# S5 first states behind the first head's group norm on GpSimd, fewer VectorE operations for the S5 parameters, the last chunk's transfers ahead of weight loads, and a different split in the tail

## The chip, the cores and the metric

The program runs on one NeuronCore of a Trainium2 chip. A core has a matrix engine (TensorE, PE in the profile), three engines for elementwise work (VectorE or DVE, ScalarE or ACT, GpSimd or POOL), and a queue engine (SyncE, SP) that only issues transfers. Each engine works through its own list of instructions; they are tied together by semaphores. The metric is device time in microseconds (us), median of repeated runs. A second, profiled execution has its own time and leaves a trace of every instruction.

## The reference

One decoder layer over 256 prompt positions and 64 sample positions (8 sequences of 8), 320 columns in all, width 2048, all in float32:

```python
proj = rms_norm(x, norm_mix) @ w_in                  # 2048 -> 5120: u | q | k | v | g
# S5: 64 groups x 64 complex states, zero-order hold
lam_bar = exp(lam * dt);  b_bar = ((lam_bar - 1) / lam) * b
bu = einsum(u, b_bar);  bu[0] += lam_bar * x0        # x0 is given for the samples
xs = associative_scan(lam_bar, bu)
y  = gelu(Re(C xs) + d * u);  y = y * sigmoid(y @ w_glu + b_glu)
# retention: 8 heads, rotary, decay per head, group norm, swish gate
o  = ((q k^T) * mask) v + (q r) * decay;  o = norm(o) * gn_w * silu(g)
x  = x + concat(y, o) @ w_out
x  = x + (silu(h2 @ w_gate) * (h2 @ w_up)) @ w_ffn_out   # h2 = rms_norm(x); 2048 -> 5632 -> 2048
y_out = rms_norm(x)                                  # also returned: S5 and retention states
```

The S5 parameters that the change touches are small: `exp(lam * dt)` per state, its powers up to the fourth, and `(lam_bar - 1) / lam`, on tiles of 128 partitions by 32 pairs of groups.

## The kernel before

Activations lie transposed, features on partitions and the 320 positions along the free dimension. Every weight block is split into two parts, `hi` (rounded to the matrix engine's fast float32 form) and `lo` (the rest), and so are the activations; a product is three matmuls (hi by hi, hi by lo, lo by hi). So each weight load of 512 KB (eight blocks of 128 by 128) costs one transfer into `raw`, one ACT cast to `hi` (L133), one DVE subtraction to `lo` (L135) and 24 matmuls of 320 columns. `raw`, `hi` and `lo` have three buffers each: a transfer waits until the `lo` three loads earlier is made, a cast waits until PE has finished with the load three earlier.

The opening (L922 to L956) multiplies four column blocks together while x arrives. It goes in steps over the 16 row blocks k of x: the first two steps take one k each, then seven take two. In a step SP loads x and w_in, ACT makes `xhi` (L272), casts the weights (`hi<-raw`, L943) and squares x for the norm (L277), DVE makes `xlo` and `lo` (L273, L944), and PE does 12 matmuls per k (L953). Behind it follow the other projections, head by head: q, k, v and g for retention and one block of u for S5. Beside them run the S5 chunks (eight, `s5_chunk`), the rotary and mask work of the heads (`head_k`, `head_v`), then the output projection, the gated unit and the feed-forward part, which is most of the time.

The S5 parameters are made beside the opening. POOL computes two exponentials from a polynomial (`s5_exps`, `vexp`, L346 to L367): first the step size, then the magnitude `rr`, 23 operations of 128 by 32 each. DVE computes sine and cosine (`s5_params`), then `lp` (powers of lam_bar), `ff`, `gp` and `r4`, the fourth power of `rr` (`s5_params2`, `s5_params3`). `first_states` puts lam_bar^4 times x0 into `lx0` with six POOL operations.

The order on PE and POOL is the order in which the code is written (a simulated clock, `clk`, and a heap of generators decide when a helper's code is run). The order on ACT, DVE and SP is made by a scheduler from priorities (`tc.high_priority(offset=...)`) and its own estimates of time; `tc.issue_after(ins)` puts an instruction behind another one of the same engine only. In the tail (from L1358) all engines go in written order.

Towards the end of the projections the last S5 chunks pass data through DRAM and inside SBUF: `back` and `yc` bring a chunk's output into channel order (L678, L683), and six small transfers `toe<-toe` (L649) copy a Toeplitz block to other partitions, after an ACT copy (L645). The PE group `py` (L104) needs `toe`. These transfers stand on SP between the loads of w_out. In the tail, the last rows of the feed-forward output are made in token layout; `scale` and `store` write the outputs, and `keep_warm(12)` puts 12 matmuls without use in front of the last broadcast.

Of the kernel before, what the change touches and what calls it, by code (L numbers as in the profile page):

```python
# [46 lines left out]
def hybrid_kernel(ctx, tc, xT, w_in, w_in4, w_out, w_glu, w_fi, w_fo, w_fot, gfr, vecs, s5p, bc, x0,  # L47
# [335 lines left out]
    def s5_params(dt_):  # L383
        newscr(0)

        ang = T(she)
        tt(ang[:, 0], prm[:, 1], dt_, MUL)
        ts(ang[:, 1], ang[:, 0], 8.0, MUL)
        ts(ang[:, 2], ang[:, 0], 64.0, MUL)
        nn = ts(T(she), ang, float(1 / np.pi), MUL, MAGIC, ADD)  # L390
        ts(nn, nn, MAGIC, SUB)
        for part in PI_PARTS:
            stt(ang, nn, -part, ang, MUL, ADD)
        par = ts(T(she), nn, 0.5, MUL, MAGIC, ADD)
        ts(par, par, MAGIC, SUB)
        stt(par, nn, 0.5, par, MUL, SUB)
        tt(par, par, par, MUL)
        ts(par, par, -8.0, MUL, 1.0, ADD)
        a2 = tt(T(she), ang, ang, MUL)
        q = T(she)  # L400
        ts(q, a2, 1.0 / factorial(13), MUL, -1.0 / factorial(11), ADD)
        for kk in (9, 7, 5, 3, 1):
            tt(q, q, a2, MUL)
            ts(q, q, (1.0 if (kk // 2) % 2 == 0 else -1.0) / factorial(kk), ADD)
        tt(q, q, ang, MUL)
        tt(es[:, 0::3], q, par, MUL)
        q = T(she)
        ts(q, a2, -1.0 / factorial(14), MUL, 1.0 / factorial(12), ADD)
        for kk in (10, 8, 6, 4, 2, 0):
            tt(q, q, a2, MUL)  # L410
            ts(q, q, (1.0 if (kk // 2) % 2 == 0 else -1.0) / factorial(kk), ADD)
        tt(ec[:, 0::3], q, par, MUL)
        for l in range(2):
            n = (NE - 1 - l + 2) // 3
            c_, s_ = ec[:, l::3][:, :n], es[:, l::3][:, :n]
            u1, u2 = T([P, n, NPAIR]), T([P, n, NPAIR])
            tt(u1, c_, c_, MUL)
            tt(u2, s_, s_, MUL)
            tt(ec[:, l + 1::3][:, :n], u1, u2, SUB)
            stt(es[:, l + 1::3][:, :n], c_, 2.0, s_, MUL, MUL)  # L420
        s5_turns(ec, es)

    def s5_params2(used):
        newscr(1)
        scr[1] = used
        tt(lp[:, 0, 0], rr, ec[:, 0], MUL)
        tt(lp[:, 1, 0], rr, es[:, 0], MUL)
        den = tt(T(sh), prm[:, 0], prm[:, 0], MUL)
        d2 = tt(T(sh), prm[:, 1], prm[:, 1], MUL)
        tt(den, den, d2, ADD)  # L430
        rden = T(sh)
        dve.reciprocal(rden, den)
        rot_t["rden"] = rden

    def s5_params3():
        rden = rot_t["rden"]
        nr = ts(T(sh), lp[:, 0, 0], -1.0, ADD)
        t1 = tt(T(sh), nr, prm[:, 0], MUL)
        t2 = tt(T(sh), lp[:, 1, 0], prm[:, 1], MUL)
        tt(t1, t1, t2, ADD)  # L440
        tt(ff[:, 0], t1, rden, MUL)
        t3 = tt(T(sh), lp[:, 1, 0], prm[:, 0], MUL)
        t4 = tt(T(sh), nr, prm[:, 1], MUL)
        tt(t3, t3, t4, SUB)
        tt(ff[:, 1], t3, rden, MUL)
        r2 = tt(T(sh), rr, rr, MUL)
        tt(r4, r2, r2, MUL)

        def cmul(o, a, b, shape, tt=tt):

            u1, u2 = T(shape), T(shape)
            tt(u1, a[0], b[0], MUL)
# [6 lines left out]
        def ri(t, i):
            return (t[:, 0, i], t[:, 1, i])  # L460

        def rep_(t, n):
            return tuple(t[:, q].unsqueeze(1).to_broadcast([P, n, NPAIR]) for q in range(2))

        cmul(ri(lp, 1), ri(lp, 0), ri(lp, 0), sh)
        cmul(ri(lp, slice(2, 4)), rep_(lp[:, :, 1], 2), ri(lp, slice(0, 2)), [P, 2, NPAIR])
        cmul(ri(gp, slice(0, 3)), rep_(ff, 3), ri(lp, slice(0, 3)), [P, 3, NPAIR])

        def b8(a):
            return a.unsqueeze(2).to_broadcast(shx)  # L470

        def first_states():

            yield max(0.0, T0 + 12.0 - clk.now)
            newscr(0)
            cmul((lx0[:, 0], lx0[:, 1]), (x0t[:, 0], x0t[:, 1]), (b8(lp[:, 0, 3]), b8(lp[:, 1, 3])), shx,
                 pool.tensor_tensor)

        spawn(first_states())
# [99 lines left out]
    def s5_chunk(c):  # L579
# [63 lines left out]
                       start=q == 0, stop=q == 1, tile_position=(0, 64 * u))  # L643
        with tc.high_priority(offset=EVAC):
            act.copy(toe[:, :, CH - 1], pk_[:, 0:64].rearrange("p (q h) -> p q h", h=16))  # L645
        for u in range(2):
            for t in range(CH - 1):
                d = 16 * (CH - 1 - t)
                sp.dma_start(toe[64 * u + d:64 * u + 64, :, t], toe[64 * u:64 * u + 64 - d, :, CH - 1])  # L649
# [30 lines left out]
        for j in range(4):  # L680
            for g in range(2):
                r = 32 * j + 16 * g
                sp.dma_start(yc[r:r + 16], back[j % 2, :, :, j // 2, g].rearrange("t h c -> h t c"))  # L683
# [60 lines left out]
    def head_v(h, v_, qg, rt, R):  # L744
# [47 lines left out]
        pool.tensor_scalar(w_, w_, -0.5, 1.5, MUL, ADD)  # L792
        pool.tensor_tensor(y_, y_, w_, MUL)
        pool.tensor_tensor(w_, m_, y_, MUL)
# [561 lines left out]
    with tail_order:  # L1356
        act.activation(wn[:, 0:1], ones[:, 0:1], AF.Sqrt)
        ps0 = ps_tok("ps_t0")  # L1358
        mm3(ps0, 0, P, range(0, 5))
        pss = norm_ps("ps_s3")  # L1360
        for i, (s, m) in enumerate(TILES):
            pe.matmul(pss[0:m, i:i + 1], acc3[:, s:s + m], ones[:, 0:1], start=True, stop=True)
        for i, (s, m) in enumerate(TILES):
            ts(sm3[0:m, i:i + 1], pss[0:m, i:i + 1], float(D * EPS), ADD)
        mm3(ps0, 0, P, range(5, FCT))
        ps1 = ps_tok("ps_t1")
        chain(0, ps0)
# [24 lines left out]
        act.copy(rbt[1], pb1[:, 0:P])
        scale(dve, 1, 0, 5, pb1)
        scale(pool, 1, 5, 10, rbt[1])
        tok_out(1, tp_o[1], sp)
        store(1, 0, 5)
        keep_warm(12)
        x_, g_ = xo[0][0:ms_], xg[0][0:ms_]
        tt(x_, psb[0:ms_, 0:TC], xt[0:ms_, 2], ADD)
        act.activation(sqj[0:ms_], x_, AF.Square, accum_out=rs[0:ms_, 2:3])  # L1400
        scale(dve, 1, 10, NF, pb1)
        store(1, 5, 10)
        store(1, 10, NF)
# [113 lines left out]
```

## Time and profile before

| | |
|---|---|
| three runs | 1428.19, 1428.51, 1429.81 us (median 1428.51) |
| the profiled execution's own time | 1427.82 us |
| its span, first to last instruction | 1426.0 us |
| busy share DVE, ACT, POOL | 67%, 43%, 9% |
| DMA | 267.07 MB moved, mean 187 GB/s |
| granted clock of TensorE | 0.999 |

The trace has one row for each instruction, or for a few like ones in sequence: its start in us from the start of the span, its duration, engine, line, operation, the tiles written and read, their shapes, how many instructions are merged, and in brackets how long the engine had been idle before it and who ended that. "ACTq" or "SPq" marks the queue side of an engine: a transfer is issued there and lands later. Overlapping durations on one engine are pipelining, so the step from one start to the next is the cost of one.

### The profile page before, as it was taken

How to read it: one execution, taken by the hardware profiler on the slowest of the kernel's cores; microseconds unless marked ns; L12 is line 12 of the kernel's file. 1: busy time of each engine (PE TensorE's matmuls, PEld its weight loads, DVE VectorE, ACT ScalarE, POOL GpSimd, SP SyncE). 2: the span in 40 equal slices, each digit the busy share in tenths (PEclk: the TensorE clock that was granted, in tenths of full speed). 3: DMA queues.
4: the chain of work that ended last, by engine and by line, in shares of the span. 5: the costliest groups of instructions: out<-in, count | busy, mean ns of one | idle time of the engine just before them, and what ended most of it. 6: DMA issues, size and time to landing. Idle time of an engine off the chain costs nothing.

```text
span 1426.0 us, 26198 instructions
## 1 busy us (share of the span) xinstructions
PE 1416.9 (99%) x10376; PEld 1406.4 (99%) x10376; DVE 958.0 (67%) x1852; ACT 606.4 (43%) x965; POOL 124.6 (9%) x194
## 2 busy tenths in 40 slices
PE   9999999999999999999999999999999999999998
PEld 8999999999999999999999999999999999999998
DVE  7978888787657756777777545767744677645453
ACT  7645555555445443333333333333333333333452
POOL 7530021110000000000001000000000000000002
PEclk9999999999999999999999999999999999999999
DMA  8555555556544466675656446666545765455442
GB/s 289 172 170 167 159 174 154 172 163 205 169 154 149 164 207 229 222 254 199 245 201 236 136 147 240 233 213 240 167 144 183 252 230 188 154 165 179 150 142 74
DMA packets 102315, 267.07 MB, mean 187 GB/s; under 512 B 27376, under 2 KB 42160, under 8 KB 102192
## 3 DMA queue, kind: packets, MB, share of 16 engines
q1 hardware_dynamic: 101824, 264.91, 55.9%
q8 instruction: 81, 1.33, 0.4%
q10 hardware_dynamic: 368, 0.49, 0.1%
q14 instruction: 42, 0.34, 0.1%
HBM read 254.44 MB, written 10.52 MB: 186 GB/s over the span
## 4 chain that ended last, share of the span: by engine, by line
PE 76%; DVE 1%; issue 0%; ACT 0%; DMA 0%; SPq 0%; DVEq 0%; ACTq 0%
PE ps_fu L146 7%; PE ps_fg L146 7%; PE ps_fg L145 7%; PE ps_fu L145 7%; PE ps_fg L147 7%; PE ps_fu L147 7%; PE ps_fo L146 7%; PE ps_fo L145 7%; PE ps_fo L147 7%; PE ps_o L145 2%; PE ps_o L147 2%; PE ps_o L146 2%; PE ps_t L1315 1%; PE ps_g L147 1%; PE ps_g L145 1%; PE ps_g L146 1%
## 5 line engine op out<-in xcount | busy, mean ns | idle before, releaser
L133 ACT CAST hi<-raw 128x1024 fp32r<-128x1024 f32 (+1 forms) x410 | 397.8, 971 | 680.9 <-PE ps_fg L146 184.8
L135 DVE TENSOR_TENSOR lo<-raw,hi 128x1024 fp32r<-128x1024 f32 (+1 forms) x410 | 462.2, 1128 | 303.9 <-ACT hi L133 301.8
L147 PE MATMUL ps_fg<-hhi,lo 128*128 128x320 f32 x704 | 217.5, 309 | 0.0
L145 PE MATMUL ps_fg<-hhi,hi 128*128 128x320 f32 x704 | 217.5, 309 | 0.0
L146 PE MATMUL ps_fg<-hlo,hi 128*128 128x320 f32 x704 | 217.5, 309 | 0.0
L146 PE MATMUL ps_fu<-hlo,hi 128*128 128x320 f32 x704 | 217.5, 309 | 0.0
L145 PE MATMUL ps_fu<-hhi,hi 128*128 128x320 f32 x704 | 217.5, 309 | 0.0
L147 PE MATMUL ps_fu<-hhi,lo 128*128 128x320 f32 x704 | 217.5, 309 | 0.0
L145 PE MATMUL ps_fo<-ahl,hi 128*128 128x320 f32 x671 | 207.6, 309 | 0.0
L146 PE MATMUL ps_fo<-ahl,hi 128*128 128x320 f32 x671 | 207.3, 309 | 0.0
L147 PE MATMUL ps_fo<-ahl,lo 128*128 128x320 f32 x671 | 207.3, 309 | 0.0
L145 PE MATMUL ps_p<-xhi,hi 128*128 128x320 f32 x560 | 177.3, 317 | 0.0
L147 PE MATMUL ps_p<-xhi,lo 128*128 128x320 f32 x560 | 173.0, 309 | 0.0
L146 PE MATMUL ps_p<-xlo,hi 128*128 128x320 f32 x560 | 172.8, 309 | 0.0
L147 PEld LDWEIGHTS ps_fg<-hhi,lo 128*128 128x128 f32 x704 | 132.1, 188 | 0.0
L146 PEld LDWEIGHTS ps_fg<-hlo,hi 128*128 128x128 f32 x704 | 132.1, 188 | 0.0
L145 PEld LDWEIGHTS ps_fu<-hhi,hi 128*128 128x128 f32 x704 | 132.1, 188 | 0.0
L146 PEld LDWEIGHTS ps_fu<-hlo,hi 128*128 128x128 f32 x704 | 132.1, 188 | 0.0
L147 PEld LDWEIGHTS ps_fu<-hhi,lo 128*128 128x128 f32 x704 | 132.1, 188 | 0.0
L145 PEld LDWEIGHTS ps_fg<-hhi,hi 128*128 128x128 f32 x704 | 132.1, 188 | 0.0
L146 PEld LDWEIGHTS ps_fo<-ahl,hi 128*128 128x128 f32 x671 | 126.0, 188 | 0.0
L145 PEld LDWEIGHTS ps_fo<-ahl,hi 128*128 128x128 f32 x671 | 125.9, 188 | 0.0
(497 smaller groups left out, 2118.2 us busy)
## 6 DMA issues: line engine op xcount, KB each, us to landing
raw<-w_fi SPq DMA_DIRECT2D x176, 512.0 KB, 4.2
raw<-w_in SPq DMA_DIRECT2D x79, 512.0 KB, 4.1
raw<-w_fo SPq DMA_DIRECT2D x61, 512.0 KB, 3.4
raw<-w_out SPq DMA_DIRECT2D x32, 512.0 KB, 3.7
hi<-vd SPq DMA_DIRECT2D x32, 512.0 KB, 5.5
lo<-vd SPq DMA_DIRECT2D x32, 512.0 KB, 5.2
raw<-w_fo SPq DMA_DIRECT2D x61, 192.0 KB, 2.4
rt<-r SPq DMA_DIRECT2D x8, 512.0 KB, 5.6
```

The lines of the kernel that those rows point to most:

```text
L133: cast = act.copy(hi[:, :m], raw[:, :m])
L135: last_lo[0] = dve.tensor_tensor(lo[:, :m], raw[:, :m], f(hi[:, :m]), SUB)
L145: pe.matmul(ps, hi, xhi[:, k], start=k == 0, stop=False)
L146: pe.matmul(ps, hi, xlo[:, k], start=False, stop=False)
L147: pe.matmul(ps, lo, xhi[:, k], start=False, stop=k == nk - 1)
L1315: pe.matmul(ps[0:m, 0:TC], a3[:, x_, k, s:s + m], w_[:, k], start=k == 0 and x_ == 0 and w_ is whi, stop=k == FCT - 1 and w_ is wlo)
```

## The change

Five edits:

1. `s5_params`: the polynomials of sine and cosine use one fused operation per term (`stt`, scalar_tensor_tensor) in place of two.
2. `s5_params2` and `s5_params3`: the two squares for `den` move from DVE to ACT, and so do both squarings that make `r4` from `rr`; the first of them reads `rr` directly. The subtraction of 1 is fused, and the complex products are done on both parts together (`cpow`).
3. `first_states` is no longer put on the heap with a due time, but called inside head 0's group norm, behind its last POOL operation.
4. Chunk 7's six `toe` transfers and chunk 6's eight `yc` transfers get a priority of 3 x 1500.
5. Tail: the second token tile is scaled and stored in pieces of 4, 5 and 4 blocks in place of 5, 5 and 3, and 10 warm matmuls stand in place of 12.

```diff
@@ s5_params
-        q = T(she)
-        ts(q, a2, 1.0 / factorial(13), MUL, -1.0 / factorial(11), ADD)
-        for kk in (9, 7, 5, 3, 1):
-            tt(q, q, a2, MUL)
-            ts(q, q, (1.0 if (kk // 2) % 2 == 0 else -1.0) / factorial(kk), ADD)
-        tt(q, q, ang, MUL)
-        tt(es[:, 0::3], q, par, MUL)
...
+        tt(ang, ang, par, MUL)
+        for dst, top, last in ((es, 13, ang), (ec, 14, par)):
+            q = ts(T(she), a2, (-1.0) ** (top // 2) / factorial(top), MUL)
+            for kk in range(top - 2, 1, -2):
+                stt(q, q, (-1.0) ** (kk // 2) / factorial(kk), a2, ADD, MUL)
+            stt(dst[:, 0::3], q, 1.0, last, ADD, MUL)
@@ s5_params2
-        den = tt(T(sh), prm[:, 0], prm[:, 0], MUL)
-        d2 = tt(T(sh), prm[:, 1], prm[:, 1], MUL)
+        den, d2 = T(sh), T(sh)
+        act.activation(den, prm[:, 0], AF.Square)
+        act.activation(d2, prm[:, 1], AF.Square)
+        act.activation(r4, rr, AF.Square)
+        act.activation(r4, r4, AF.Square)
@@ s5_params3
-        nr = ts(T(sh), lp[:, 0, 0], -1.0, ADD)
-        t1 = tt(T(sh), nr, prm[:, 0], MUL)
+        t1 = stt(T(sh), lp[:, 0, 0], -1.0, prm[:, 0], ADD, MUL)
...
-        r2 = tt(T(sh), rr, rr, MUL)
-        tt(r4, r2, r2, MUL)
...
+        def cpow(o, a, b, n):
+            used = scr[1]
+            shn = [P, 2, n, NPAIR]
+            u1, u2 = (T([P, 2 * n, NPAIR]).rearrange("p (r n) j -> p r n j", r=2) for _ in range(2))
+            for u, q in ((u1, 0), (u2, 1)):
+                tt(u, a, b[:, q].unsqueeze(1).unsqueeze(1).to_broadcast(shn), MUL)
+            tt(o[:, 0], u1[:, 0], u2[:, 1], SUB)
+            tt(o[:, 1], u1[:, 1], u2[:, 0], ADD)
+            scr[1] = used
...
         def first_states():
-
-            yield max(0.0, T0 + 12.0 - clk.now)
             newscr(0)
...
-        spawn(first_states())
+        rot_t["first"] = first_states
@@ s5_chunk
-        for u in range(2):
-            for t in range(CH - 1):
...
+        with tc.high_priority(offset=3 * EVAC if c == 7 else 0):
+            for u in range(2):
+                for t in range(CH - 1):
+                    d = 16 * (CH - 1 - t)
+                    sp.dma_start(toe[64 * u + d:64 * u + 64, :, t], toe[64 * u:64 * u + 64 - d, :, CH - 1])
...
+        with tc.high_priority(offset=3 * EVAC if c == 6 else 0):
+            for j in range(4):
+                for g in range(2):
+                    r = 32 * j + 16 * g
+                    sp.dma_start(yc[r:r + 16], back[j % 2, :, :, j // 2, g].rearrange("t h c -> h t c"))
@@ head_v, behind the last pool operation of the group norm
+        if h == 0:
+            rot_t["first"]()
@@ tail
-        scale(dve, 1, 0, 5, pb1)
-        scale(pool, 1, 5, 10, rbt[1])
+        scale(dve, 1, 0, 4, pb1)
+        scale(pool, 1, 4, 9, rbt[1])
...
-        keep_warm(12)
+        keep_warm(10)
...
-        scale(dve, 1, 10, NF, pb1)
+        scale(dve, 1, 9, NF, pb1)
```

In all DVE has 22 instructions fewer and ACT four more; PE has two fewer (the warm matmuls) and is otherwise in the same order. `s5_params2` is called inside `tc.issue_after(turned.ins)`, where `turned` is a DVE instruction; for the four new ACT instructions that sets no place. The scheduler's order shows where they came to stand. These are ACT's rows in the opening before, from the two `xhi` of k = 10 and 11 (the first two rows) to the step of k = 12 and 13; the bracket names the semaphores that a row waits for (DMAHW are transfers):

```order
L272 ACTIVATE xhi<-retp,vec 128x320 [waits DMAHW6_49]
L272 ACTIVATE xhi<-retp,vec 128x320
L943 CAST hi<-raw 128x1024 [waits DMAHW7_49,PE_49]
L272 ACTIVATE xhi<-retp,vec 128x320 [waits DMAHW0_49]
L272 ACTIVATE xhi<-retp,vec 128x320
L277 ACTIVATE retp<-retp 128x640 [waits DVE_49]
L943 CAST hi<-raw 128x1024 [waits DMAHW1_49,PE_49]
```

and the same piece of ACT's order now:

```order
L272 ACTIVATE xhi<-retp,vec 128x320 [waits DMAHW6_49]
L272 ACTIVATE xhi<-retp,vec 128x320
L424 ACTIVATE r_126<-rr 128x32 [waits Pool_49]
L942 CAST hi<-raw 128x1024 [waits DMAHW7_49,PE_49]
L425 ACTIVATE r_126<-r_126 128x32 [waits Activation_49]
L272 ACTIVATE xhi<-retp,vec 128x320 [waits DMAHW0_49]
L272 ACTIVATE xhi<-retp,vec 128x320
L277 ACTIVATE retp<-retp 128x640 [waits DVE_49]
L942 CAST hi<-raw 128x1024 [waits DMAHW1_49,PE_49]
```

The first squaring of `rr` (L424; `r_126` is `r4`) now stands ahead of the weight cast for k = 10 and 11 and waits for POOL, which writes `rr`; the squares for `den` (L422, L423, not shown) stand two steps earlier and wait for the transfer of `prm`. On POOL, between head 0's group norm (its last two rows first) and head 1's k, the order before was

```order
L793 TENSOR_TENSOR gy<-gy 128x2
L794 TENSOR_TENSOR gy<-mv,gy 128x2
L867 COPY qsp<-q__1059 128x64
L452 TENSOR_TENSOR scrt<-x0t,lp 128x256
L453 TENSOR_TENSOR scrt<-x0t,lp 128x256
L454 TENSOR_TENSOR lx_133<-scrt 128x256
L455 TENSOR_TENSOR scrt<-x0t,lp 128x256
L456 TENSOR_TENSOR scrt<-x0t,lp 128x256
L457 TENSOR_TENSOR lx_133<-scrt 128x256
L880 TENSOR_TENSOR kvf<-k__1142,kdt 128x64
L882 COPY ksp<-k__1142 128x64
```

The six rows from L452 to L457 are the first states. Now POOL's order there is

```order
L790 TENSOR_TENSOR gy<-gy 128x2
L791 TENSOR_TENSOR gy<-mv,gy 128x2
L445 TENSOR_TENSOR scrt<-x0t,lp 128x256
L446 TENSOR_TENSOR scrt<-x0t,lp 128x256
L447 TENSOR_TENSOR lx_133<-scrt 128x256
L448 TENSOR_TENSOR scrt<-x0t,lp 128x256
L449 TENSOR_TENSOR scrt<-x0t,lp 128x256
L450 TENSOR_TENSOR lx_133<-scrt 128x256
L866 COPY qsp<-q__1047 128x64
L879 TENSOR_TENSOR kvf<-k__1124,kdt 128x64
L881 COPY ksp<-k__1124 128x64
```

where only the copy of head 1's q has changed its place, behind all six. On SP, from the end of the projections to the third load of w_out and beyond, the order before was

```order
L683 DMA yc<-back 16x4x80
L132 DMA raw<-w_out 128x1024
L683 DMA yc<-back 16x4x80 x2
L132 DMA raw<-w_out 128x1024
L683 DMA yc<-back 16x4x80 x2
L132 DMA raw<-w_out 128x1024
L683 DMA yc<-back 16x4x80 x3
L649 DMA toe<-toe 16x4x16
L649 DMA toe<-toe 32x4x16
L649 DMA toe<-toe 48x4x16
L132 DMA raw<-w_out 128x1024
L649 DMA toe<-toe 16x4x16
```

(two more `toe` transfers follow), and is now

```order
L680 DMA yc<-back 16x4x80 x8
L132 DMA raw<-w_out 128x1024
L645 DMA toe<-toe 16x4x16
L645 DMA toe<-toe 32x4x16
L645 DMA toe<-toe 48x4x16
L645 DMA toe<-toe 16x4x16
L645 DMA toe<-toe 32x4x16
L645 DMA toe<-toe 48x4x16
L132 DMA raw<-w_out 128x1024 x4
```

so that the second to fifth load of w_out stand behind all six `toe` transfers.

More of the change, by code (lines that the diff above doesn't have):

```diff
@@ L399, in s5_params @@
         a2 = tt(T(she), ang, ang, MUL)
-        q = T(she)
-        ts(q, a2, 1.0 / factorial(13), MUL, -1.0 / factorial(11), ADD)
-        for kk in (9, 7, 5, 3, 1):
-            tt(q, q, a2, MUL)
-            ts(q, q, (1.0 if (kk // 2) % 2 == 0 else -1.0) / factorial(kk), ADD)
-        tt(q, q, ang, MUL)
-        tt(es[:, 0::3], q, par, MUL)
[L407 to L412, printed above, removed]
+        tt(ang, ang, par, MUL)
[4 more added lines that the diff above has]
+            stt(dst[:, 0::3], q, 1.0, last, ADD, MUL)
         for l in range(2):
@@ L442, in s5_params3 @@
         t3 = tt(T(sh), lp[:, 1, 0], prm[:, 0], MUL)
-        t4 = tt(T(sh), nr, prm[:, 1], MUL)
+        t4 = stt(T(sh), lp[:, 0, 0], -1.0, prm[:, 1], ADD, MUL)
         tt(t3, t3, t4, SUB)
         tt(ff[:, 1], t3, rden, MUL)
-        r2 = tt(T(sh), rr, rr, MUL)
-        tt(r4, r2, r2, MUL)
         def cmul(o, a, b, shape, tt=tt):
@@ L457, in cmul @@
             tt(o[1], u1, u2, ADD)
[L459 to L467, printed above, removed]
+        def cpow(o, a, b, n):
[7 more added lines that the diff above has]
+            scr[1] = used
+        cpow(lp[:, :, 1:2], lp[:, :, 0:1], lp[:, :, 0], 1)
+        cpow(lp[:, :, 2:4], lp[:, :, 0:2], lp[:, :, 1], 2)
+        cpow(gp, lp[:, :, 0:3], ff, 3)
         def b8(a):
@@ L645, in s5_chunk @@
             act.copy(toe[:, :, CH - 1], pk_[:, 0:64].rearrange("p (q h) -> p q h", h=16))
-        for u in range(2):
-            for t in range(CH - 1):
-                d = 16 * (CH - 1 - t)
-                sp.dma_start(toe[64 * u + d:64 * u + 64, :, t], toe[64 * u:64 * u + 64 - d, :, CH - 1])
+        with tc.high_priority(offset=3 * EVAC if c == 7 else 0):
[3 more added lines that the diff above has]
+                    sp.dma_start(toe[64 * u + d:64 * u + 64, :, t], toe[64 * u:64 * u + 64 - d, :, CH - 1])
         with tc.high_priority(offset=2 * EVAC if c == 7 else 0):
@@ L679, in s5_chunk @@
         yc = s5.tile([P, CH, NC], F32, name="yc", tag="yc", bufs=1)
[L680 to L683, printed above, removed]
+        with tc.high_priority(offset=3 * EVAC if c == 6 else 0):
[3 more added lines that the diff above has]
+                    sp.dma_start(yc[r:r + 16], back[j % 2, :, :, j // 2, g].rearrange("t h c -> h t c"))
         yield DL["y"]
@@ L1392, in hybrid_kernel @@
         act.copy(rbt[1], pb1[:, 0:P])
-        scale(dve, 1, 0, 5, pb1)
-        scale(pool, 1, 5, 10, rbt[1])
+        scale(dve, 1, 0, 4, pb1)
+        scale(pool, 1, 4, 9, rbt[1])
         tok_out(1, tp_o[1], sp)
-        store(1, 0, 5)
-        keep_warm(12)
+        store(1, 0, 4)
+        keep_warm(10)
         x_, g_ = xo[0][0:ms_], xg[0][0:ms_]
@@ L1400, in hybrid_kernel @@
         act.activation(sqj[0:ms_], x_, AF.Square, accum_out=rs[0:ms_, 2:3])
-        scale(dve, 1, 10, NF, pb1)
-        store(1, 5, 10)
-        store(1, 10, NF)
+        scale(dve, 1, 9, NF, pb1)
+        store(1, 4, 9)
+        store(1, 9, NF)
         pool.tensor_tensor(g_, x_, grow[0:ms_], MUL)
```

## The prediction

> **What bounds the kernel now.** I read the busy shares first, then the waits of PE, then tables by stage. The page's first part, four rows of the table by stretch (stretch, its length, then busy time and instruction count of PE, PEld, DVE, ACT, POOL, then clock and DMA), and what PE waited for:
>
> ```profile
> PE 1416.9 (99%) x10376; PEld 1406.4 (99%) x10376; DVE 958.0 (67%) x1852; ACT 606.4 (43%) x965; POOL 124.6 (9%) x194
> ...
> 26.00:42.00 16.00, 16.00 (x114) 16.00 (x113) 15.66 (x57) 7.78 (x19) 12.13 (x26) 1.00 0.81 268
> 42.00:66.00 24.00, 23.94 (x168) 23.69 (x167) 23.28 (x75) 15.86 (x37) 16.07 (x30) 1.00 0.48 158
> ...
> 344.00:1400.00 1056.00, 1056.00 (x7204) 1055.87 (x7203) 667.47 (x1214) 407.08 (x533) 25.50 (x8) 1.00 0.57 193
> 1400.00:1426.00 26.00, 20.51 (x119) 19.16 (x117) 9.41 (x27) 6.53 (x18) 7.14 (x6) 0.97 0.29 102
> ...
> PE pss L104 <- POOL ksp L882: 0.9, 1, 0.9
> PE py L953 <- ACT hi L943: 0.6, 1, 0.6
> PE py L104 <- DMA toe<-toe: 0.5, 1, 0.5
> ```
>
> PE is busy 1416.9 of 1426.0 us, and for 1056 us on end it runs one matmul per 0.147 us (1056 / 7204). So an edit can gain only what stands in PE's few waits and in the tail, about 2 us here; but whatever stops PE anywhere is lost in full, since nothing later runs below its pace. The question for each edit is therefore whether PE waits less or more. From 26 to 66 us DVE is nearly full as well (15.66 of 16, then 23.28 of 24).
>
> **The new wait on ACT.** The order of the change puts the first squaring of `rr` on ACT ahead of the weight cast for k = 10 and 11, and `rr` is the last thing POOL makes from its exponentials. Rows of the timeline (start, duration, what), for ACT, PE and POOL:
>
> ```profile
> 17.19 1.05 ACT L943 CAST hi<-raw 128x1024 fp32r<-128x1024 f32 x1 [0.84 <-DMA raw<-w_in]
> ...
> 18.79 1.00 ACT L272 ACTIVATE xhi<-retp,vec 128x320 fp32r<-128x320 f32 x2
> 19.69 1.03 ACT L943 CAST hi<-raw 128x1024 fp32r<-128x1024 f32 x1
> ...
> 24.12 0.31 PE L953 MATMUL py<-xhi,hi 128*128 128x320 f32 x1
> ...
> 20.72 0.29 POOL L346 TENSOR_SCALAR scrt<-scrt 128x32 f32<-128x32 f32 x1
> 21.09 1.02 POOL L361 TENSOR_TENSOR scrt<-scrt 128x32 f32<-128x32 f32 x1
> ...
> 33.38 0.25 POOL L361 TENSOR_TENSOR scrt<-scrt 128x32 f32<-128x32 f32 x1
> 33.72 0.30 POOL L346 TENSOR_SCALAR scrt<-scrt 128x32 f32<-128x32 f32 x1
> ...
> 39.41 0.33 POOL L367 TENSOR_TENSOR rr<-scrt 128x32 f32<-128x32 f32 x1
> ...
> 20.76 1.25 DVE L944 TENSOR_TENSOR lo<-raw,hi 128x1024 fp32r<-128x1024 f32 x1 [0.24 <-ACT hi L943]
> ```
>
> ACT comes to the squaring when the `xhi` pair is done, at 19.79; `rr` was ready at 39.74. The two squares for `den` two steps earlier (POOL reads the same `prm` well before) cost at most 0.2 us each by the 128x32 forms, and the 0.84 us that ACT idled before 17.19 takes them up. Behind the squaring stand the casts and `xhi` of k = 10 to 15; behind those on DVE `lo` and `xlo`, and on SP the next weight loads, which wait for buffers.
>
> An engine passes nothing that waits: POOL's copy of head 1's q (below) sat 8.26 us waiting, with first-state products behind it whose inputs were there. So ACT stands until `rr` comes.
>
> When will that be? POOL has 30 operations from 20.72 to `rr`, and took 19.0 us. Its long ones end with a long two-input DVE operation: the one at 21.09 took 1.02 us and ended at 22.11, DVE's `lo` at 22.01; the same form at 33.38, beside small DVE operations, took 0.25, with steps of 0.34 and 0.38 us. Now DVE stands still too, having no cast to subtract from once its `xlo` is done at 20.5. I take 0.34 us a step: 30 x 0.34 = 10.3, so `rr` at about 31.0. The ends are 0.29 a step (the shortest of the exponentials' steps; 29.4) and no relief (39.7). [...]
>
> Then 0.2 us for the squaring and 1.03 for the cast: PE's k = 10, which began at 24.12 (the PE row), can begin at 32.3. **PE stands 8.2 us.** After a stop PE may start slowly:
>
> ```profile
> 1.12 3.65 PE L118 MATMUL warm_ps<-ones 128*128 128x512 f32 x8 [1.12 <-POOL ones L64]
> ...
> 1417.22 2.92 PE L118 MATMUL warm_ps<-ones 128*128 128x512 f32 x12
> ...
> 39.55 0.21 DVE L184 SCALAR_TENSOR_TENSOR ry<-rt,ry 128x3 f32<-128x3 f32 x1
> ...
> 41.51 0.83 PE L104 MATMUL ps_r<-ident,ry 128*128 128x128 f32 x6
> ```
>
> The same matmul cost 0.456 us at the program's start (3.65 / 8) and 0.243 in the tail (2.92 / 12). Eight such slow ones are 1.7 us, my price for a cold restart; its lower end is zero. The granted clock doesn't show this. [...] It matters little, for DVE sets a floor of its own: it resumes at 32.3 instead of 20.76, 11.55 us late, and was busy nearly without a break from there to the norm's root `ry` at 39.76 (15.66 of 16 us in the table). With one parameter operation fewer ahead of that, `ry` comes at about 51.2, while PE wants it at 41.51 plus its delay. So PE's delay is at least 9.7 us; with the cold start it is 8.2 + 1.7 = **9.9 us**. I take 9.9.
>
> **Fewer DVE operations.** Of the 22, eleven lie in the sine and cosine:
>
> ```profile
> L180 DVE TENSOR_TENSOR scrt<-scrt 128x96 f32<-128x96 f32 x14 | 3.5, 263 | 0.0
> L184 DVE SCALAR_TENSOR_TENSOR scrt<-scrt 128x96 f32<-128x96 f32 x4 | 1.0, 266 | 0.0
> ```
>
> By these groups (count, busy us, mean ns) the fused form costs what one plain operation does (1.0 / 4 and 3.5 / 14, 0.25 us each). Some 1.9 us fall away before head 0's rotary work and about as much after; PE waited for none of it, so it is worth nothing by itself. It serves to catch up the 1.6 us by which DVE is later than PE after the stop (11.55 less 9.9).
>
> **First states earlier.** Rows of POOL, PE and DVE:
>
> ```profile
> 66.16 0.53 POOL L794 TENSOR_TENSOR gy<-mv,gy 128x2 f32<-128x2 f32 x1
> 74.94 3.85 POOL L867 COPY qsp<-q__1059 128x64 f32<-128x64 f32 x1 [8.26 <-DVE q__1059 L180]
> 78.75 0.63 POOL L452 TENSOR_TENSOR scrt<-x0t,lp 128x256 f32<-128x256 f32 x1
> ...
> 85.36 0.24 POOL L882 COPY ksp<-k__1142 128x64 f32<-128x64 f32 x1
> ...
> 62.78 0.22 DVE L180 TENSOR_TENSOR lp<-scrt 128x64 f32<-128x64 f32 x1
> ...
> 79.77 0.81 DVE L180 TENSOR_TENSOR k__1142<-k__1142,sw 128x320 f32<-128x320 f32 x1
> ...
> 85.65 0.49 PE L104 MATMUL pss<-qsp,ksp 128*128 128x128 f32 x2 [0.93 <-POOL ksp L882]
> ```
>
> The products ran from 78.75 to 85.1, 6.4 us, between the copies of q and k; `lp` was ready at 63.0. In POOL's idle stretch from 66.7 they end by 73.1, before q comes. Then q's copy, even at 3.85 us, ends by 78.8, and k's copy follows its data at 80.6, ended by 81.2, against PE's need at 84.7. So PE gains its 0.93 us; all these times move alike by the delay above. Lower end: nothing, if POOL is held up until k's copy is late again.
>
> **Transfers ahead of weight loads.** Rows of SP, ACT and PE, and the landing times of w_out's loads (KB, median us):
>
> ```profile
> 326.42 0.33 SPq L132 DMA_DIRECT2D raw<-w_out  x1
> ...
> 328.37 0.35 SPq L132 DMA_DIRECT2D raw<-w_out  x1
> ...
> 338.73 2.35 SPq L649 DMA_DIRECT2D toe<-toe  x3
> ...
> 331.45 0.21 ACT L645 COPY toe<-pk__4711 128x64 f32<-128x64 f32 x1 [0.81 <-PE pk__4711 L104]
> ...
> 342.74 0.42 PE L104 MATMUL py<-kst,toe 64*64 64x80 f32 x10 [0.45 <-DMA toe<-toe]
> ...
> 343.72 0.41 PE L163 MATMUL ps_o<-r4a,hi 128*128 128x320 f32 x1
> ...
> raw<-w_out SPq DMA_DIRECT2D x32, 512.0 KB, 3.7
> ```
>
> The last three `toe` were issued only at 338.73, behind a load that waited for a buffer. Now all six go at 331.7, when ACT's copy is made, and take some 4.5 us to issue: landed by 339, the 0.45 us go. The new cost: SP stands from about 327 to 331.7 with loads two to five behind it, so load two goes at 336.2 and not 328.37. It lands at 339.9, cast and subtraction (1.03 + 1.25) make it 342.2; PE wants it after the first load's 12 matmuls, at 343.7 + 1.8 - 0.45 = 345.0. Covered by 2.8 us; a landing 3 us longer would start to cost. So -0.45, with ends of -0.45 and +1.
>
> **Tail.** Two DVE rows; the warm matmuls (1417.22) are quoted above:
>
> ```profile
> 1416.85 0.81 DVE L1350 TENSOR_TENSOR ahl<-x,ps_b 128x640 f32<-128x640 f32 x1
> ...
> 1419.33 0.40 DVE L184 SCALAR_TENSOR_TENSOR ahl<-ahl 64x1 f32<-64x1 f32 x2
> ```
>
> The root of the last tile is ready at 1419.73, but PE's warm matmuls hold the broadcast until 1420.08. Two fewer free PE 0.48 us earlier, at 1419.6; the piece of 512 in place of 640 columns shortens DVE by about 0.15 and the root comes at 1419.6. So -0.45, and what follows is unchanged; at worst nothing.
>
> **Sum.** +9.9 - 0.93 - 0.45 - 0.45 = +8.1 us on 1427.82 gives 1435.9. The median of the runs is 0.7 above the profiled execution, so the forecast is **1436.6 us**, slower by 0.57%.
>
> **Rivals.**
> - *POOL gets no relief* and `rr` stays at 39.74: PE's delay grows by 8.7, to 1445.3. For it: the step may have other causes than DVE. Against: the long operations end with DVE's. One in ten, with all between.
> - *DVE stays behind after the stop*: head 0's k or a `lo` is late for PE, 2 to 5 us more, 1439 to 1442. For it: DVE is 97% busy there and 1.6 us behind. Against: 1.9 us of its work fall away at that place. One in ten.
> - *The wait doesn't reach PE*, the case that is not slower. It holds if `rr` is made by 22.8 (24.12 less cast and squaring): then only the gains remain, 1428.5 - 1.8 = 1426.7. POOL would need 30 operations in 2.1 us, 0.07 each, against 0.29 at the least; or ACT would have to run past the squaring. 0.07.
> - *The change does not do what it says*: first states as late as before, `toe` covered by another wait; the forecast is then 1437 to 1438, inside its own range.
>
> **How the numbers follow.** Forecast 0.73 (own range 1434.0 to 1438.5, by the ends of the POOL step, the restart and the gains), POOL without relief 0.10, DVE behind 0.10, not slower 0.07. The range takes in the first three: 1433.8 to 1445.3. A measurement of this kernel tells about 0.2% (2.9 us) from no change; the gains alone, 1.8 us, lie within that, so the last case counts as 0.05 same and 0.02 faster, and slower is 0.93.
>
> **What would show it.** ACT idle some 11 us before L424, ended by POOL `rr`; PE idle about 8 us around 24 to 32 for `hi` (L942), then matmuls at twice their step for some 3 us; POOL's steps near 0.34 in that stretch; no wait of `pss` on `ksp` or of `py` on `toe`; the broadcast 0.45 us sooner after the last product. An ACT that does not wait there, or a PE that makes up time later, would prove the argument wrong.

## The result and the profile after

The changed kernel takes 1438.15 us (median of 6 runs, 1437.45 to 1440.58), the kernel before, timed beside it, 1428.35 us (6 runs, 1427.92 to 1429.81). The ratio is 1.0069 with a 95% interval of 1.0056 to 1.0082: the change costs 9.8 us. The profiled execution took 1437.45 us with a span of 1435.4 (before: 1427.82 and 1426.0).

From the page, the table by stretch and the waits of PE after the change (columns as in the prediction):

```profile
PE 1419.4 (99%) x10374; PEld 1408.9 (98%) x10374; DVE 955.6 (67%) x1830; ACT 606.4 (42%) x969; POOL 112.2 (8%) x194
```

```profile
24.00:34.00 10.00, 1.97 (x7) 1.98 (x8) 2.00 (x3) 3.19 (x7) 5.46 (x22) 0.66 0.00 1
34.00:42.00 8.00, 8.00 (x45) 8.00 (x45) 8.00 (x11) 6.01 (x12) 0.00 (x0) 0.79 0.80 264
342.00:1400.00 1058.00, 1057.54 (x7253) 1056.93 (x7253) 675.98 (x1237) 409.31 (x542) 25.97 (x8) 1.00 0.58 194
```

```profile
PE py L952 <- ACT hi L942: 8.1, 1, 8.1
...
PE ps_o L164 <- DVE r4b L180: 0.5, 1, 0.5
PE pst L109 <- DVE k__728 L180: 0.3, 1, 0.3
PE pst L109 <- ACT kd L723: 0.3, 1, 0.3
```

PE is busy 99% of the span as before, so the share says nothing. The stretch from 24 to 34 us does: PE busy for 1.97 of 10 us, no DMA, and little work on any engine but POOL. In the next stretch PE is fully busy and yet starts only 45 matmuls in 8 us (59 in the same stretch before), at a granted clock of 0.79. The old waits for `ksp` and `toe` are gone from the list, and three new ones of 0.3 to 0.5 us are there. (`pst` are the transposes of head 0's k and v, `kd` is its transposed k times the decay, `pss` the scores of a head, `ps_o` the output projection, and `r4a` and `r4b` are the split retention outputs of the first and the last four heads, which it reads.)

The chain of the stop, from the timelines of ACT, POOL and PE (start, duration, what, idle before and its releaser):

```profile
18.16 1.00 ACT L272 ACTIVATE xhi<-retp,vec 128x320 fp32r<-128x320 f32 x2
30.81 0.23 ACT L424 ACTIVATE r<-rr 128x32 f32<-128x32 f32 x1 [11.65 <-POOL rr L367]
30.95 1.03 ACT L942 CAST hi<-raw 128x1024 fp32r<-128x1024 f32 x1
...
20.90 0.26 POOL L361 TENSOR_TENSOR scrt<-scrt 128x32 f32<-128x32 f32 x1
...
30.52 0.25 POOL L367 TENSOR_TENSOR rr<-scrt 128x32 f32<-128x32 f32 x1
...
23.57 0.31 PE L952 MATMUL ps_p<-xhi,lo 128*128 128x320 f32 x1
32.03 0.64 PE L952 MATMUL py<-xhi,hi 128*128 128x320 f32 x1 [8.15 <-ACT hi L942]
...
34.06 0.47 PE L952 MATMUL ps_p<-xlo,hi 128*128 128x320 f32 x1
34.33 0.47 PE L952 MATMUL py<-xhi,lo 128*128 128x320 f32 x1
...
37.26 0.39 PE L952 MATMUL ps_p<-xlo,hi 128*128 128x320 f32 x1
37.49 0.30 PE L952 MATMUL py<-xhi,lo 128*128 128x320 f32 x1
```

ACT is through with `xhi` at 19.16 and idles 11.65 us before a squaring of 0.23 us, until POOL's `rr` is made at 30.77. The weight cast that PE wants stands right behind it. The last rows show the second loss: from 32.03 to 37.26 matmuls start 0.27 us apart (34.06 and 34.33), and only then 0.147 as before.

Where PE's time went can be read by setting each matmul's start against the start of the same matmul before (both from the timelines of PE; every number is a difference of two such starts):

| place | start before | start after | later by | step there |
|---|---|---|---|---|
| k = 2, first product | 9.86 | 9.45 | -0.40 | the run's own start |
| k = 10, first product | 24.12 | 32.03 | 7.91 | stop, +8.3 |
| end of the slow matmuls | 26.91 | 37.26 | 10.35 | half rate, +2.44 |
| head 0's k transposes | 52.73 | 63.65 | 10.92 | k late on DVE, +0.57 |
| head 0's v transposes | 53.83 | 64.98 | 11.15 | kd late on ACT, +0.23 |
| head 1's `pss` | 85.65 | 95.72 | 10.06 | wait for ksp gone, -1.09 |
| last chunk's `py` | 342.74 | 352.02 | 9.27 | wait for toe gone, -0.58 (and 0.2 on the way) |
| `ps_o` on `r4b` | 347.49 | 357.29 | 9.79 | new wait, +0.52 (0.62 there, 0.1 won on the way) |
| last broadcast | 1420.08 | 1429.54 | 9.46 | tail, -0.33 |

The first row is not the change's doing: in the profiled executions of the other kernels below, the same start lies between 0.45 us earlier and 1.38 later than before. So the stop is 8.31 us, from -0.40 to 7.91.

The table is the frame for the experiments: is the stop one wait, is it the whole loss, and what are the other edits worth once it is away?

### The profile page after: what moved, and what is told of

The parts are those of the page before. It is cut to its first block, busy times and chain, and to the rows that moved or that the text cites. A ratio compares the mean times of both kernels' runs of the same rounds, so it can differ in the third digit from the quotient of the medians.

```text
span 1435.4 us, 26173 instructions
## 1 busy us (share of the span) xinstructions
PE 1419.4 (99%) x10374; PEld 1408.9 (98%) x10374; DVE 955.6 (67%) x1830; ACT 606.4 (42%) x969; POOL 112.2 (8%) x194
## 4 chain that ended last, share of the span: by engine, by line
PE 95%; POOL 1%; DVE 1%; issue 1%; DMA 1%; ACT 0%; SPq 0%; DVEq 0%; ACTq 0%
PE ps_fu L147 7%; PE ps_fg L147 7%; PE ps_fg L145 7%; PE ps_fu L145 7%; PE ps_fu L146 7%; PE ps_fg L146 7%; PE ps_fo L146 7%; PE ps_fo L147 7%; PE ps_fo L145 7%; PE ps_p L145 5%; PE ps_p L146 5%; PE ps_p L147 5%; PE ps_o L145 2%; PE ps_o L146 2%; PE ps_o L147 2%; PE ps_t L1314 1%
```

## The experiments

### The stop: the squarings of rr elsewhere, and alone

In the first kernel the two squarings keep their engine and lose their place: they go behind ACT's copy of the broadcast norm.

```diff
-            act.copy(rbc, rps)
+            rot_t["rbc"] = act.copy(rbc, rps)
...
-        act.activation(r4, rr, AF.Square)
-        act.activation(r4, r4, AF.Square)
+        with tc.issue_after(rot_t["rbc"].ins):
+            act.activation(r4, rr, AF.Square)
+            act.activation(r4, r4, AF.Square)
```

> The changed kernel with one thing moved: the two squarings of rr on ACT are put behind ACT's copy of the broadcast norm (rbc), that is behind all weight casts of the first projection; nothing is left out. Theory (the stop at k=10 is the whole loss, through ACT's order): ACT no longer idles 11.65 us at L424, PE no longer stands 8.2 us before k=10, runs at no half rate after it, and head 0's k and v are in time. Of the end's +9.35 us the stop's +7.91, the half rate's +2.44 and the k and v waits' +0.80 go, and -1.8 is left: about 1426.5 us, 1.8 us (0.13%) under the kernel before. Rival 1 (the loss comes from the longer list of squarings, powers and first states on DVE and POOL, and the wait on ACT only shows it): the time stays at 1434 or above. Rival 2 (DVE, relieved of the stop, is late for head 0's k anyway): 1427.5 to 1429, with a wait of the k transposes above 0.5 us.

Measured: 1427.23 us (11 runs) against 1428.41 for the kernel before, ratio 0.9994 (0.9985 to 1.0003). The 9.8 us are gone, and what remains of the change can't be told from no change. Two waits of PE in this kernel, ACT's first squaring, and PE's first product of k = 10:

```profile
PE ps_o L164 <- DVE r4b L180: 0.4, 1, 0.4
PE pst L109 <- DVE k__728 L180: 0.3, 1, 0.3
```

```profile
42.26 0.23 ACT L425 ACTIVATE r<-rr 128x32 f32<-128x32 f32 x1
...
23.68 0.31 PE L953 MATMUL py<-xhi,hi 128*128 128x320 f32 x1
```

The squaring runs without an idle moment before it, and PE's k = 10 begins at 23.68, without a wait. The first rival (a longer list on DVE and POOL) falls. The second was half right: a wait for k is there (0.3 us), without any stop, so it isn't the stop's doing. It has a run of its own below.

The second kernel is the kernel before with nothing but these two squarings on ACT where the change puts them (and DVE's two products for r4 left off, which they replace).

```diff
+        act.activation(r4, rr, AF.Square)
+        act.activation(r4, r4, AF.Square)
...
-        r2 = tt(T(sh), rr, rr, MUL)
-        tt(r4, r2, r2, MUL)
```

> The kernel before with only the two squarings of rr moved from DVE to ACT at the place they have in the changed kernel; nothing else is changed, nothing left out. Theory: this alone makes the stop. ACT reaches the squaring at 19 to 20 us and waits for POOL's rr, the cast of the weights for k=10,11 behind it comes 8 to 9 us late, PE stands for 8 us and then runs at half rate for 5 us: the stop's 8 plus 2.4 plus 0 to 1.5 for DVE, 1438.5 to 1440.5 us, above the changed kernel since nothing is won back later. Rival (the stop needs the shorter DVE lists or the moved first states too): within 1 us of the kernel before, or a stop below 4 us.

Measured: 1439.08 us (4 runs), ratio 1.0078 (1.0064 to 1.0092), inside what the theory said.

```profile
30.98 0.23 ACT L431 ACTIVATE r<-rr 128x32 f32<-128x32 f32 x1 [11.06 <-POOL rr L367]
...
32.20 0.64 PE L953 MATMUL py<-xhi,hi 128*128 128x320 f32 x1 [7.54 <-ACT hi L943]
...
37.97 0.63 PE L953 MATMUL pb<-xhi,lo 128*128 128x320 f32 x2
```

Two squarings of 0.23 us make the stop by themselves; the changed kernel, with all its edits, is about a microsecond faster (0.9 by medians). Set against the kernel before as in the table, PE is 8.08 us late at k = 10 and 10.88 at 38.2: half rate cost 2.80 us here and lasted 6 us. DVE still has the long parameter list of before, and yet there is no wait for k.

### Half rate after the stop

Here 34 matmuls of no use keep PE busy through the stop; ACT waits as in the changed kernel.

```diff
+        if k0 == 10:
+            keep_warm(34)
```

> The changed kernel, with 34 matmuls of no use put on PE ahead of k=10 so that PE is busy during the stop (about 8.3 us of them at 0.243 us); ACT's wait stays, nothing is left out. Theory A (the half rate after the stop costs its 2.4 us outright): matmuls run at 0.147 us from k=10 on and the time falls by 2.4 us, to 1435.7. Theory B (DVE sets the floor: head 0's k is ready at 63.6 us whatever PE does before, since DVE's lo chain starts with the late cast): PE reaches the k transposes 2.4 us earlier and waits there 2.4 us longer (0.34 becomes 2.7), and the time stays at 1438.1 plus or minus 0.4. By the prediction's own floor (9.7 us of DVE against 9.9 of PE) it would be B.

Measured: 1445.14 us (4 runs), ratio 1.0117 (1.0103 to 1.0130). Neither theory. The table by stretch and the timelines say why:

```profile
24.00:34.00 10.00, 9.59 (x47) 7.89 (x46) 0.56 (x1) 1.76 (x5) 6.57 (x26) 1.00 0.00 1
49.00:60.00 11.00, 9.94 (x39) 9.54 (x40) 7.80 (x17) 3.69 (x5) 8.42 (x13) 0.54 0.57 177
```

```profile
33.45 0.41 PE L954 MATMUL py<-xhi,hi 128*128 128x320 f32 x1 [0.41 <-ACT hi L942]
...
34.00 0.31 PE L954 MATMUL ps_p<-xhi,hi 128*128 128x320 f32 x1
34.15 0.31 PE L954 MATMUL py<-xlo,hi 128*128 128x320 f32 x1
...
49.70 0.64 PE L145 MATMUL ps_pv<-xhi,hi 128*128 128x320 f32 x1 [5.34 <-ACT hi L133]
...
59.08 0.36 PE L145 MATMUL ps_pv<-xhi,hi 128*128 128x320 f32 x1
...
46.47 2.12 ACT L592 ACTIVATE cz<-raw_bc 64x64 f32<-64x64 f32 x8 [6.18 <-DMA raw_bc<-bc]
48.61 2.94 ACT L133 CAST hi<-raw 128x1024 fp32r<-128x1024 f32 x3
```

The first half is what was asked. With PE kept busy, the granted clock is 1.00 through the stop, and from k = 10 on matmuls start 0.15 us apart at once, where in the changed kernel, whose PE idled, they start 0.27 us apart at a clock of 0.50; so the half rate there comes from the idling. The second half is a matter of order: with the added matmuls in the program, the scheduler placed the `cz` operations, which wait for a transfer, ahead of the casts for head 0's v (`ps_pv`); in the changed kernel three of these casts run before them. ACT stood for 6.18 us before them, PE for 5.34, and then ran at half rate a second time (0.27 us apart, clock 0.54), for 9.4 us with short waits and small matmuls among them. So what the half rate is worth at the end of the program, and whether DVE's floor would have taken it, stays open. But the run repeats the change's own fault by accident: an operation that waits was put ahead of a cast that PE needs.

### The edits around the stop

The next runs take the other edits alone. First states on POOL, in the kernel before:

```diff
-            yield max(0.0, T0 + 12.0 - clk.now)
             newscr(0)
...
-        spawn(first_states())
+        rot_t["first"] = first_states
...
+        if h == 0:
+            rot_t["first"]()
```

> The kernel before with only the first states moved behind head 0's group norm on POOL; nothing is left out. Theory: no stop at k=10, the wait of pss for ksp (0.93 us) is gone and nothing late takes its place: the span 0.9 to 1.1 us below the kernel before, about 1427.3 us in one look. Rival (the first states delay POOL's group norm or the next ksp): a wait of another head's pss or of the S5 chunk appears, and the span is that of the kernel before.

Measured: a single run, 1428.45 us, span 1426.6 (before 1426.0). The wait for `ksp` is gone, and something late has taken its place. DVE's and POOL's rows here:

```profile
68.87 1.11 DVE L180 TENSOR_TENSOR m<-raw_bc,lpc 128x512 f32<-128x512 f32 x1
69.90 1.65 DVE L135 TENSOR_TENSOR lo<-raw,hi 128x1024 fp32r<-128x1024 f32 x1
...
70.43 1.61 POOL L456 TENSOR_TENSOR scrt<-x0t,lp 128x256 f32<-128x256 f32 x1
...
71.61 0.42 PE L147 MATMUL ps_p<-xhi,lo 128*128 128x320 f32 x1 [0.70 <-DVE lo L135]
75.87 0.41 PE L147 MATMUL ps_p<-xhi,lo 128*128 128x320 f32 x1 [0.46 <-DVE lo L135]
```

and the same two operations of DVE in the kernel before, with POOL idle:

```profile
68.06 0.69 DVE L180 TENSOR_TENSOR m<-raw_bc,lpc 128x512 f32<-128x512 f32 x1
68.67 1.22 DVE L135 TENSOR_TENSOR lo<-raw,hi 128x1024 fp32r<-128x1024 f32 x1
```

POOL's idle stretch wasn't free. Its products now run beside DVE's: `m` takes 1.11 us instead of 0.69, `lo` 1.65 instead of 1.22, POOL's own product up to 1.61. PE falls 1.56 us behind by 75.9 and gets 0.91 back at `pss`: +0.65 alone, in one profiled execution; the whole time can't be told from the 1428.46 of the kernel before, timed beside it. The rival held in part: a late wait takes back the gain, at a place that it hadn't named.

The shorter DVE list alone, in the kernel before, with the squarings where they do no harm (behind the `rbc` copy); its edits are those of the change to the S5 parameters.

> The kernel before with the DVE part of the change alone (fewer operations for the S5 parameters, the squarings of rr on ACT behind the rbc copy); first states, transfers and tail stay as before; nothing is left out. Theory (the shorter DVE list earns nothing by itself; it only pays for what is put beside it): the wait of pss for ksp stays at 0.6 to 1.0 us, a wait of the transposes for k of 0.3 to 1.2 us is new, DVE's lo casts at 70 to 76 us are 1 to 2 us earlier than in the run with only the first states moved and PE doesn't wait for them: the span 0.3 us below to 1.0 us above the kernel before. Rival (fewer DVE operations bring PE time): a span 0.5 us or more below it, with no new wait.

Measured: 1428.13 us (10 runs), ratio 0.9998 (0.9988 to 1.0007). The time is the theory's and so is the new wait for k, but the wait for `ksp` isn't there:

```profile
49.08 1.29 DVE L180 TENSOR_TENSOR qg<-q__718,gqt 128x32 f32<-128x32 f32 x2
...
50.55 1.66 DVE L135 TENSOR_TENSOR lo<-raw,hi 128x1024 fp32r<-128x1024 f32 x1
...
73.31 0.50 POOL L865 COPY qsp<-q__1041 128x64 f32<-128x64 f32 x1 [8.20 <-DVE q__1041 L180]
...
81.82 0.23 POOL L880 COPY ksp<-k__1124 128x64 f32<-128x64 f32 x1
...
54.08 0.41 PE L109 MATMUL pst<-ident,k__728 128*128 128x128 f32 x2 [0.75 <-DVE k__728 L180]
```

With DVE ahead, head 1's q comes to POOL at 73.3 instead of 74.9 and its copy takes 0.50 us instead of 3.85, so `ksp` is made by 82.1 and not 85.6, with the first states still in the old place. Against the kernel before, PE gains 1.09 us at `pss` and loses 0.92 at head 0's k and 0.23 at its v. Either edit alone takes the 0.93 us away, each at its own price; together they gain it once.

The wait for k comes from DVE's order. The change lets `lp`, a sum, head 0's `qg` and the reciprocal run ahead of the `lo` and the k behind it. The next kernel builds on the first and puts `qg`, `lp` and what follows from them behind head 0's k:

```diff
-        with tc.issue_after(turned.ins):
-            s5_params2(exps[1])
...
         k_ = rot(ps, "k_")
+        if not h:
+            with tc.issue_after(rot_t["k"].ins):
+                scale_q(0)
+                s5_params2(exps[1])
```

(`scale_q` is the loop that makes `qg`; `rot_t["k"]` is the rotary's last sum.)

> As the run that moves the squarings behind the rbc copy, and in addition head 0's scaled queries (qg) and the S5 parameters behind the pole (lp, den, rden) stand behind head 0's rotary of k in DVE's order instead of ahead of it; nothing is left out. Theory (the k wait of 0.3 to 1.2 us in the runs without the stop comes from what the change put ahead of k on DVE: lp, den's sum, qg and the reciprocal, 0.52+0.51+1.29+0.34 us, ahead of lo and k): k is ready over 1 us earlier, the waits of the transposes for k (0.3 to 1.2) are gone, that for v's kd may stay at 0.3; 0.3 to 0.8 us below the run that moves only the squarings, 1426.4 to 1427. Rival (POOL's new neighbourhood, which stretches DVE's lo to 1.66 and k's sum to 0.82, is the cause): the wait stays at 0.3 or more.

Measured: 1426.85 us (11 runs), ratio 0.9989 (0.9980 to 0.9998). Two of the three waits of PE that are left beside the program's start:

```profile
PE py L961 <- ACT hi L951: 0.8, 1, 0.8
...
PE ps_o L164 <- DVE r4b L180: 0.2, 1, 0.2
```

Both waits of the transposes are gone, though `lo` and the k sum are still stretched (1.44 and 0.82 us; 1.22 and 0.48 in the kernel before). So it was the order. Of the 0.3 to 0.8 us expected the medians give 0.4 (1427.23 and 1426.85, each timed beside its own runs of the kernel before); the spans are equal (1424.3 and 1424.4), as this run's own start was later (0.8 us of waits for the first casts).

### Transfers ahead of the weight loads

Three orders of SP's queue on top of the moved squarings. First without the new priorities:

```diff
-        with tc.high_priority(offset=3 * EVAC if c == 7 else 0):
...
-        with tc.high_priority(offset=3 * EVAC if c == 6 else 0):
```

> As the run that moves the squarings behind the rbc copy, but without the new priorities of the yc and toe transfers (SP's order as in the kernel before); nothing is left out. Theory: the wait of py for toe is back (0.58 us by the ledger), the wait of ps_o for r4b (0.52 us) is gone, so the change of SP's order gives and takes the same: within 0.2 us of the run that moves only the squarings. Rival (the priorities are worth their -0.45 us and the r4b wait has another cause): 0.5 us slower than that run, with both waits in the trace.

Measured: 1427.58 us (11 runs), ratio 1.0000 (0.9990 to 1.0009), 0.35 above the run that only moves the squarings, a little more than the 0.2 expected, and the intervals of the two overlap. The wait for `toe` is back (0.57 us) and the one for `r4b` gone, as the theory had it; head 0's k is waited for 1.22 us in this profile, against 0.3 there, which this edit doesn't touch and which isn't explained.

Then with priority for the `yc` transfers alone:

```diff
-        with tc.high_priority(offset=3 * EVAC if c == 7 else 0):
+        with tc.high_priority(offset=0 if c == 7 else 0):
```

> As the run that moves the squarings behind the rbc copy, and in addition the last chunk's toe copies lose their priority while the yc transfers of the chunk before keep theirs: SP's queue now reads yc x8, w_out x3, toe x4, w_out, toe x2; nothing is left out. Theory (the new 0.5 us wait for r4b comes from the w_out loads that stand behind the toe copies, whose casts hold ACT's queue): the wait of ps_o for r4b goes, the toe copies still are 3 us earlier than before the change unless the last two fall behind the fourth load, so py waits for toe 0 to 0.6 us: 0 to 0.5 us below the run that moves only the squarings. Rival (r4b is late because of DVE's own order, not of ACT's queue): the r4b wait stays at 0.4 to 0.5 us and the time is that of the other run or up to 0.6 us above it.

Measured: 1428.03 us (11 runs), ratio 0.9997 (0.9989 to 1.0006). The `r4b` wait goes, as said, but two `toe` copies stand behind a load that waits for a buffer, and PE waits 1.45 us for them: a miss, above the upper end.

Last, priority for the `toe` copies alone, on top of the order that puts k first, so that three loads go ahead of all six `toe` copies and the fourth behind:

```diff
-        with tc.high_priority(offset=3 * EVAC if c == 7 else 0):
+        with tc.high_priority(offset=EVAC if c == 7 else 0):
...
-        with tc.high_priority(offset=3 * EVAC if c == 6 else 0):
-            for j in range(4):
+        for j in range(4):
```

> As the run that puts k first, and in addition the yc transfers lose their new priority while the last chunk's toe copies keep one: SP's queue reads yc, w_out, yc x2, w_out, yc x2, w_out, toe x6, yc x2, w_out; nothing is left out. Theory (the r4b wait comes from load two being behind the toe copies, the toe wait from the last toe copies being behind load four): here three loads are ahead of the toe copies and the fourth behind, so both the waits for toe (0.5 to 1.4) and for r4b (0.4) are gone: 0.4 us below the run that only puts k first, about 1426. Rival: a wait for y of the chunk before, whose yc transfers now come 4 us later, takes their place: same or slower than that run.

Measured: 1426.40 us (11 runs), ratio 0.9987 (0.9979 to 0.9996). SP's queue, ACT's casts and PE at that place in the changed kernel:

```profile
332.94 5.06 SPq L680 DMA_DIRECT2D yc<-back  x8
...
341.65 3.85 SPq L645 DMA_DIRECT2D toe<-toe  x6
345.60 7.61 SPq L132 DMA_DIRECT2D raw<-w_out  x4
...
350.55 1.05 ACT L133 CAST hi<-raw 128x1024 fp32r<-128x1024 f32 x1 [3.34 <-DMA raw<-w_out]
...
352.81 1.18 ACT L1058 CAST r4b<-retp 128x320 fp32r<-128x320 f32 x3
...
357.29 0.41 PE L164 MATMUL ps_o<-r4b,hi 128*128 128x320 f32 x1 [0.46 <-DVE r4b L180]
```

and in this one (all about 11 us earlier), with the row of its table by stretch from 342 us on:

```profile
330.71 0.35 SPq L132 DMA_DIRECT2D raw<-w_out  x1
331.16 3.85 SPq L646 DMA_DIRECT2D toe<-toe  x6
...
340.73 1.05 ACT L133 CAST hi<-raw 128x1024 fp32r<-128x1024 f32 x1 [2.10 <-issue]
341.68 1.18 ACT L1064 CAST r4b<-retp 128x320 fp32r<-128x320 f32 x3
```

```profile
342.00:1400.00 1058.00, 1058.00 (x7216) 1057.95 (x7216) 669.71 (x1217) 408.30 (x538) 25.61 (x8) 1.00 0.59 193
```

In the changed kernel load two leaves SP at 345.60 and ACT idles 3.34 us for it with the casts of `r4b` queued behind. In this one the third of three loads has gone at 330.71, ahead of `toe`, and neither `toe` nor `r4b` is waited for. From 342 to 1400 us PE is busy for 1058.00 of 1058 us. This is the fastest version by medians: 2.1 us under the kernel before, 11.8 under the changed one. Its interval overlaps that of the order with k first, so the last 0.4 us rest on the waits that are gone.

The tail edit alone, in the kernel before:

```diff
-        keep_warm(12)
+        keep_warm(10)
```

(and the cuts at 4 and 9 in place of 5 and 10).

> The kernel before with only the tail edit (10 in place of 12 warm-up matmuls, the scaled columns cut at 4 and 9 in place of 5 and 10); nothing is left out. Theory: all start times of PE as in the kernel before until the tail, and there the transposes of the last token block start 0.3 to 0.5 us earlier (by the changed kernel's ledger 0.33): the span 0.3 to 0.45 us shorter from the same start. Rival (the stores set the end): the transposes come earlier and the end doesn't, 0 to 0.1 us.

Measured: a single run, 1429.13 us. This execution started 1.3 us late (the first casts waited for their transfers) and its span is longer by that; at the end PE is 1.74 us behind at `pss` and 1.39 at the last broadcast, 0.35 gained, and the span ends 1.32 later than before's. The expected 0.3 to 0.45 is there, in this one execution.

## Why the prediction was right, step by step

The forecast of 1436.6 us lies 1.55 under the median of 1438.15, and the slowdown came for the reason it gave; the restart was priced too low, and two waits were not in the sum.

- **The stop.** Held nearly to the number. POOL's relief: `rr` at 30.77 (31.0 forecast), POOL's product in 0.26 us where it took 1.02 beside DVE's long operation. PE's start of k = 10 at 32.03 (32.3); it stood 8.3 us (8.2). The run with the squarings alone shows that this one wait makes it, the run with them moved that nothing else does.
- **The restart, mis-sized.** "Eight such slow ones are 1.7 us" took the program's first 3.65 us as the length of the slow time, an estimate that no run shows for a stop. It lasted 5.3 us here and cost 2.44; in the run with the squarings alone it lasted 6 and cost 2.80, and after the second stop of the run with the 34 matmuls it lasted 9.4, though PE was not always busy in them. The changed kernel's own start shows that this length isn't fixed either: there matmuls still start 0.27 us apart up to 6.51, some 5.4 us after the first at 1.12. "The granted clock doesn't show this" holds for that start, where the clock reads 1.00, and was wrong for this place: it reads 0.66 and 0.79 in the two stretches of the table, and 0.50 from 32.0 to 37.3. What sets the length was not shown.
- **DVE's floor.** Forecast: `ry` at about 51.2 and PE's delay at least 9.7. Measured: the last row of the root starts at 49.84 and lasts 0.15, so `ry` is ready at 49.99, and PE comes to it at 51.93. The floor was mis-sized by 1.2 us; DVE made up more than was said and didn't set the time at that place.
- **DVE behind at head 0's k, a rival at one in ten.** It came, at 0.80 us for k and v instead of 2 to 5, and not through the stop: the runs without a stop that keep the change's DVE order wait 0.3 to 1.2 us for k as well, and the one with k first doesn't. The sum had nothing for it, because I counted the operations that fall away and not the order of those that stay.
- **Fewer DVE operations, "worth nothing by itself".** The time agrees (0.9998), the reason not: it takes the `ksp` wait away and pays with the k wait.
- **First states earlier, -0.93.** The wait went (-1.09 in the ledger). But alone the edit costs 0.65 us by its one profile: I laid it in POOL's idle stretch and didn't ask who runs beside it on DVE, though I had just read the like off POOL's rows (1.02 us beside a long operation of DVE, 0.25 beside short ones). With the shorter DVE list beside it, as in the run that only moves the squarings, PE waits for no `lo`.
- **Transfers, -0.45.** The `toe` wait went (-0.58). The new cost was given as covered by 2.8 us, up to the weight itself; the weight was in time. What I left out is what stands behind its cast on ACT: `r4b`'s casts, +0.52 us. Together next to nothing.
- **Tail, -0.45.** Mis-sized: -0.33. Two matmuls fewer moved the last broadcast from 2.86 to 2.52 us behind the first warm one.

In sum: the stop and its restart cost 10.75 us (8.31 and 2.44), 0.85 more than the 9.9 forecast, k and v 0.80, `r4b` 0.52; this execution happened to start 0.40 earlier; the gains were 0.2 larger than forecast (-1.09, -0.58 and -0.33 against -1.83), and small parts on the way and at the end come to -0.3. That makes the 9.35 by which the span grew, against 8.1.

## What to carry to other kernels

An operation moved to an idle engine takes its wait along, and everything queued behind it waits too. Before moving one, look at when its input is ready (here 39.7 us) against when that engine gets there (19.8), and name what stands behind it; 0.23 us of work cost 10 here, and the same look behind a late weight's cast would have found the `r4b` wait. Small edits of about a microsecond are not additive: two of them removed the same wait, and one only paid because of the other, so each wants its row in a ledger of start times rather than a place in a sum.

## What the runs showed of the hardware

- After PE had stood idle for 8.2, 7.5 and 5.3 us, matmuls started 0.267 us apart instead of 0.147 for 5.3, 6 and 9.4 us (the last with short waits and small matmuls among them); with PE kept busy through the stop they started 0.15 us apart at once. The length of the slow time was a different one each time.
- POOL and DVE were slower beside each other: POOL's 128x32 product takes 0.26 us with DVE still and 1.02 beside a 128x1024 subtraction; DVE's subtraction takes 1.22 us with POOL idle and 1.65 beside POOL's 128x256 products. Which side pays differs: in the run with the shorter DVE list, the subtraction at 74.12 keeps its 1.21 us and POOL's product beside it takes 2.04. The rows give the price for both sides, and no cause.
- One 128x64 copy on POOL took 3.85 us in the kernel before and 0.50 in the run with the shorter DVE list, its data ready 1.6 us earlier. The rows show what ran beside it: before, two of DVE's 128x1024 subtractions, the second of which ends at 78.70 and the copy at 78.79; in the run with the first states alone again 3.85 us, from 77.47 to 81.32; in the run with the shorter list, only DVE operations of 0.5 us and less. That the subtractions held it up is my reading of the rows of before and of the shorter list; no run tried it.
